# Seven products of halves for the first projection of both MLPs, with the weight sums made by accumulating DMAs

## The chip, the cores and the metric

The kernel runs on one core of a Trainium2 chip. The core has a matrix engine (TensorE, PE in the profile, with its weight loads as PEld), a vector engine (VectorE, DVE), an activation engine (ScalarE, ACT), GpSimd (POOL) and SyncE (SP). SP and POOL also issue DMAs, from queues of their own. The metric is the device time of one execution in microseconds (us); lower is better.

## The reference

A trunk of two residual layers over 512 tokens of width 1024, all float32. Each layer is a token mixer and an MLP, both behind an RMS norm. Only the MLP's computation is touched:

```python
def rmsnorm(x, g):
    xf = x.astype(jnp.float32)
    y = xf * lax.rsqrt(jnp.mean(xf * xf, axis=-1, keepdims=True) + EPS)
    return (y * g.astype(jnp.float32)).astype(x.dtype)

def mlp(h, w1, w2):            # w1: 1024 x 4096, w2: 4096 x 1024
    a = jax.nn.relu(h @ w1)
    return (a * a) @ w2

for i in range(DEPTH):         # DEPTH = 2: an even mixer, then an odd one
    ...
    h = rmsnorm(x, norm_mlp[i])
    x = x + mlp(h, w1[i], w2[i])
```

## The kernel before

All activations lie transposed, features on the 128 partitions and 512 tokens along the row. A float32 product is made of three matmuls in a rounded 32-bit format: each operand is split into a high part and the remainder, and `mm3` (L124) adds high by high, high by low and low by high.

Weights come as blocks of 128 x 1024, in the order in which they are used. `block_parts` (L101) loads block i from HBM by a DMA on SP's queue into `raw` (two buffers), ACT copies it into `whi` (L111) and DVE subtracts that from `raw` into `wlo` (L112); `whi` and `wlo` have four buffers each. This is called the split of a block below. `wblock` (L119) hands out the next block and has two more under way in the program text. Apart from the even mixer, where the order of TensorE is written by hand, the framework orders the instructions of each engine when it compiles, by the order of the text and by when its model expects their operands.

An MLP (`mlp`, L301) alternates between two kinds of unit, each of two weight blocks, 48 matmuls with 512 columns into a PSUM tile of two banks:

- `m1(g)` (L319), four units for 8 of the 32 feature tiles of the hidden layer. `Norm.step` (L294) has written the inputs, x times the norm's gain, split into A[0:8] and A[8:16]. The factor of the norm per token, `rs`, comes behind the product: DVE takes max(o, 0) * rs (L326), ACT squares it (L327) and makes the high part (L329), DVE the low part (L330).
- `m2(g)` (L345), four units that multiply those 8 hidden tiles with w2 and add to x (`x_add`, L287). In the last round (g = 3) each unit is followed by the steps of the next norm, or by the store to HBM. The very last unit (`last_unit`, L332) is cut finer, and its last half into two products of 256 columns.

The order is m1(0), m1(1), m2(0), m1(2), m2(1), m1(3), m2(2), m2(3). Before an MLP stands the last projection of the mixer (units `woa` in the even one, `wo1` in the odd one), after each unit of which two steps of the MLP's norm follow.

Of the kernel before, what the change touches and what calls it, by code (L numbers as in the profile page):

```python
# [7 lines left out]
F32 = mybir.dt.float32  # L8
F32R = mybir.dt.float32r
# [10 lines left out]
WARM = 17  # L20
LAT = (4.56, 2.32, 3.03, 2.9, 2.44)
GLAT = (0.88, 0.94, 1.37, 0.54, 2.0)

V_MIX = 0
V_MLP = 16
# [19 lines left out]
def kernel(  # L45
# [45 lines left out]
    def mm_tile(name):  # L91
        return ps.tile([P, 2, S], F32, tag="mm", name=name, bufs=2)
# [4 lines left out]
    wcount = [0]  # L97
    ready = []
    AHEAD = 2

    def block_parts(n):  # L101
        i = wcount[0]
# [12 lines left out]
    def emit_block():  # L115
        for _ in block_parts(1):
            pass

    def wblock():  # L119
        while len(ready) < AHEAD + 1 and wcount[0] < w.shape[0]:  # L120
            emit_block()
        return ready.pop(0)

    def mm3(o, w_hi, w_lo, a_hi, a_lo, start, stop, swap=False):  # L124
        if swap:
            w_hi, w_lo, a_hi, a_lo = a_hi, a_lo, w_hi, w_lo
        pe.matmul(o, w_hi, a_hi, start=start, stop=False)  # L127
        pe.matmul(o, w_hi, a_lo, start=False, stop=False)  # L128
        pe.matmul(o, w_lo, a_hi, start=False, stop=stop)  # L129

    def t_unit_g(name, acts):
        o = mm_tile(name)
        n = len(acts)
        for b in range(n // 4):
            hi, lo = wblock()
            hi = hi.rearrange("p (k n) -> p k n", k=4)
            lo = lo.rearrange("p (k n) -> p k n", k=4)
            for kk in range(4):
                k = b * 4 + kk
                for j in range(2):  # L140
                    c = slice(j * P, (j + 1) * P)
                    mm3(o[:, j, :], hi[:, kk, c], lo[:, kk, c], A[:, acts[k][0], :], A[:, acts[k][1], :],
                        k == 0, k == n - 1)
                if k < n - 1:
                    yield
        return o
# [8 lines left out]
    def t_unit(name, acts):  # L155
        return drain(t_unit_g(name, acts))
# [126 lines left out]
    def bc2(t):  # L283
        return t[:, None, :].to_broadcast([P, 2, S])

    def x_add(o, n):
        dve.tensor_add(x[:, 2 * n : 2 * n + 2, :], x[:, 2 * n : 2 * n + 2, :], o)  # L287

    class Norm:
# [8 lines left out]
        def rs(self):  # L298
            return norm_rs(self.ss, self.name)

    def mlp(l, nrm, nxt):  # L301
        with ExitStack() as c2:
            mp = c2.enter_context(tc.tile_pool(name=f"mp{l}", bufs=2, reuse_waits="tile"))
            E = mp.tile([P, 16, S], F32R, tag="E", name=f"E{l}", bufs=1)
            st = {}

            def aslot(f):
                i = f % 8
                if (f // 8) % 2 == 0:
                    return A[:, 16 + i, :], A[:, 24 + i, :]  # L310
                return E[:, i, :], E[:, 8 + i, :]

            def apair(f):
                i = f % 8
                if (f // 8) % 2 == 0:
                    return A[:, 16 + i : 18 + i, :], A[:, 24 + i : 26 + i, :]
                return E[:, i : i + 2, :], E[:, 8 + i : 10 + i, :]

            def m1(g):  # L319
                for q in range(4):  # L320
                    f = 8 * g + 2 * q
                    o = t_unit(f"m1_{l}_{f}", H)
                    if "rs" not in st:
                        st["rs"] = nrm.rs()
                    r = mp.tile([P, 2, S], F32, tag="r", name=f"r_{l}_{f}")
                    dve.scalar_tensor_tensor(r, o, 0.0, bc2(st["rs"]), op0=ALU.max, op1=ALU.mult)  # L326
                    act.activation(r, r, AF.Square)  # L327
                    hi, lo = apair(f)
                    act.copy(hi, r)  # L329
                    dve.tensor_sub(lo, r, hi.bitcast(F32))  # L330

            def last_unit(g, n):  # L332
                ws = [[t.rearrange("p (k n) -> p k n", k=4) for t in wblock()] for _ in range(2)]
                for j, c0, c1 in ((0, 0, S), (1, 0, S // 2), (1, S // 2, S)):
                    c = slice(j * P, (j + 1) * P)
                    row = 2 * n + j
                    o = m_tile(f"m2_{l}_{g}_{n}_{j}_{c0}", "tp" if c0 else "s")
                    for k in range(8):
                        hi, lo = ws[k // 4]
                        ah, al = aslot(8 * g + k)  # L340
                        mm3(o[:, c0:c1], hi[:, k % 4, c], lo[:, k % 4, c], ah[:, c0:c1], al[:, c0:c1], k == 0, k == 7)
                    dve.tensor_add(x[:, row, c0:c1], x[:, row, c0:c1], o[:, c0:c1])
                    nc.sync.dma_start(out[row * P : (row + 1) * P, c0:c1], x[:, row, c0:c1])

            def m2(g):  # L345
                for n in range(4):
# [3 lines left out]
                    o = mm_tile(f"m2_{l}_{g}_{n}")  # L350
                    for b in range(2):
                        hi, lo = wblock()
                        hi = hi.rearrange("p (k n) -> p k n", k=4)
                        lo = lo.rearrange("p (k n) -> p k n", k=4)
                        for kk in range(4):
                            k = 4 * b + kk
                            ah, al = aslot(8 * g + k)
                            for j in range(2):
                                c = slice(j * P, (j + 1) * P)
                                mm3(o[:, j, :], hi[:, kk, c], lo[:, kk, c], ah, al, k == 0, k == 7)  # L360
# [8 lines left out]
            m1(0)  # L369
            m1(1)  # L370
            m2(0)
            m1(2)
            m2(1)
            m1(3)
            m2(2)
            m2(3)

    def even_mixer(nrm, nxt):
        nonlocal x
# [461 lines left out]
        plan.run(gla, fg)  # L841
        for _ in fg:
            pass
        woa = [t_unit_g(f"woa{n}", O[0:4]) for n in range(4)]
        for n in (0, 0, 1, 1):
            next(woa[n])
        for n in range(4):
            x_add(drain(woa[n]), n)
            nxt.step(2 * n)
            nxt.step(2 * n + 1)  # L850
        order.close()
        ops.close()

    def odd_mixer(nrm, nxt):
        with ExitStack() as c2:
# [44 lines left out]
            for c in range(2):  # L900
# [22 lines left out]
            for n in range(4):  # L923
                x_add(t_unit(f"wo1_{n}", O[4:8] + O[0:4]), n)
                nxt.step(2 * n)
                nxt.step(2 * n + 1)

    n0 = Norm("n0", V_MIX)
    n1 = Norm("n1", V_MLP)
    even_mixer(n0, n1)  # L930
    n2 = Norm("n2", V_MIX + 8)
    mlp(0, n1, n2)
    n3 = Norm("n3", V_MLP + 8)
    odd_mixer(n2, n3)
    mlp(1, n3, None)


def _t_block(np, w, k0, n0, width):
    per = 1024 // width
    return w[k0 : k0 + per * P, n0 : n0 + width].reshape(per, P, width).transpose(1, 0, 2).reshape(P, 1024)  # L940


def _pair(np, blocks, w, ks, n0):
    for k0 in ks:
        blocks.append(_t_block(np, w, k0, n0, 256))


def _layout(np, i):
# [8 lines left out]
            blocks.append(_t_block(np, we, 256 * b, n0, 512))  # L957

    def mlp(l):
        def m1(g):  # L960
            for q in range(4):
                _pair(np, blocks, w1[l], (0, 512), (8 * g + 2 * q) * P)

        def m2(g):
            for n in range(4):
                _pair(np, blocks, w2[l], (1024 * g, 1024 * g + 512), 256 * n)

        m1(0), m1(1), m2(0), m1(2), m2(1), m1(3), m2(2), m2(3)

    tok(kb), tok(qb), tok(vb)  # L970
    _pair(np, blocks, we, (0, 512), qa)
# [88 lines left out]
```

## Time and profile before

| | |
|---|---|
| median of 3 runs | 1088.49 us (1087.35 to 1090.71) |
| the profiled execution | 1089.53 us, of which the span from its first to its last instruction is 1087.5 us |
| mean granted TensorE clock | 0.998 of full speed |
| busy share of the span: PE, PEld, DVE, ACT, POOL | 99%, 82%, 51%, 37%, 10% |
| read from HBM, written | 101.94 MB, 2.10 MB |

The span is what the trace covers; the 2 us beside it belong to the execution's time. Matmuls are pipelined, so their durations overlap, and the pace of TensorE is read from the distance between the starts of consecutive matmuls.

### The profile page before, as it was taken

What the parts mean: (1) busy time and instruction counts of PE and PEld (TensorE: products, weight loads), DVE (VectorE), ACT (ScalarE), POOL (GpSimd) and SP (SyncE); (2) the same over time, 40 slices, a digit from 0 to 9 for tenths busy, and PEclk for the clock granted to TensorE, in tenths of its full rate; (3) what the DMA queues carried; (4) which work ended last, traced back from release to release, by engine and by line L of the source; (5) the groups of instructions that cost most, each with busy time, mean ns of one, the idle gap of its engine ahead of it and who ended that gap; (6) DMA issues with size and microseconds to landing.
All of it is one profiled execution on the core that took longest, in us unless ns stands there. A gap on an engine that the chain in (4) does not pass through costs nothing.

```text
span 1087.5 us, 12594 instructions
## 1 busy us (share of the span) xinstructions
PE 1076.5 (99%) x5008; PEld 889.8 (82%) x5008; DVE 556.0 (51%) x774; ACT 404.7 (37%) x554; POOL 113.2 (10%) x126
## 2 busy tenths in 40 slices
PE   9999999999999999999999999999999999999998
PEld 7678888688888888888888888888888888888887
DVE  6788875867444334334335774545443334344331
ACT  5465565545333133123224432334342133133110
POOL 2244523213000000000002100121000000000000
PEclk9999999999999999999999999999999999999999
DMA  7223114122222222323232322232323322323231
GB/s 230 79 78 97 59 61 152 40 78 97 97 97 97 97 97 97 97 97 97 97 97 97 107 97 89 97 98 89 99 95 99 95 99 96 97 96 99 95 112 58
DMA packets 32044, 104.84 MB, mean 96 GB/s; under 512 B 3730, under 2 KB 6259, under 8 KB 31987
## 3 DMA queue, kind: packets, MB, share of 16 engines
q1 hardware_dynamic: 31202, 101.69, 28.5%
q0 software_dynamic: 640, 2.10, 0.6%
q8 instruction: 39, 0.64, 0.3%
q10 hardware_dynamic: 144, 0.26, 0.1%
q14 instruction: 19, 0.15, 0.0%
HBM read 101.94 MB, written 2.10 MB: 96 GB/s over the span
## 4 chain that ended last, share of the span: by engine, by line
PE 89%; DVE 5%; ACT 2%; POOL 1%; DMA 1%; issue 1%; SPq 0%; POOLq 0%; DVEq 0%; ACTq 0%
PE m L129 21%; PE m L128 21%; PE m L127 21%; PE wo L129 1%; PE wo L128 1%; PE wo L127 1%; DMA raw<-in_w_dram 1%; PE av L696 1%; PE ptp L677 1%; DVE wlo L112 1%; PE va L127 1%; PE va L129 1%; PE va L128 1%; PE xc L129 1%; PE xc L127 1%
## 5 line engine op out<-in xcount | busy, mean ns | idle before, releaser
L111 ACT CAST whi<-raw 128x1024 fp32r<-128x1024 f32 (+1 forms) x188 | 194.3, 1034 | 535.9 <-PE m L128 432.0
L112 DVE TENSOR_TENSOR wlo<-raw,whi 128x1024 fp32r<-128x1024 f32 (+1 forms) x188 | 228.0, 1213 | 198.4 <-ACT whi L111 198.2
L127 PE MATMUL m<-A,whi 128*128 128x512 f32 x768 | 299.0, 389 | 0.0
L129 PE MATMUL m<-A,wlo 128*128 128x512 f32 x768 | 299.0, 389 | 0.0
L128 PE MATMUL m<-A,whi 128*128 128x512 f32 x768 | 299.0, 389 | 0.0
L128 PEld LDWEIGHTS m<-A,whi 128*128 128x128 f32 x768 | 144.2, 188 | 30.0
L127 PEld LDWEIGHTS m<-A,whi 128*128 128x128 f32 x768 | 144.2, 188 | 29.9
L129 PEld LDWEIGHTS m<-A,wlo 128*128 128x128 f32 x768 | 144.2, 188 | 29.7
L128 PE MATMUL m<-E,whi 128*128 128x512 f32 (+1 forms) x264 | 101.1, 383 | 0.0
L129 PE MATMUL m<-E,wlo 128*128 128x512 f32 (+1 forms) x264 | 101.1, 383 | 0.0
L127 PE MATMUL m<-E,whi 128*128 128x512 f32 (+1 forms) x264 | 101.1, 383 | 0.0
L287 DVE TENSOR_TENSOR x<-x,m 128x1024 f32<-128x1024 f32 x31 | 37.9, 1221 | 109.1 <-PE m L129 109.1
L326 DVE SCALAR_TENSOR_TENSOR r<-m,rs_n 128x1024 f32<-128x1024 f32 x32 | 39.2, 1225 | 96.8 <-PE m L129 96.7
L268 POOL TENSOR_TENSOR ss_n<-ss_n,sq_n 128x512 f32<-128x512 f32 x21 | 32.8, 1561 | 391.7 <-ACT sq_n L266 391.0
L127 PEld LDWEIGHTS m<-E,whi 128*128 128x128 f32 x264 | 49.6, 188 | 9.8
L128 PEld LDWEIGHTS m<-E,whi 128*128 128x128 f32 x264 | 49.6, 188 | 9.7
L129 PEld LDWEIGHTS m<-E,wlo 128*128 128x128 f32 x264 | 49.6, 188 | 9.6
L327 ACT ACTIVATE r<-r 128x1024 f32<-128x1024 f32 x32 | 34.0, 1061 | 19.9 <-DVE r L326 19.9
L330 DVE TENSOR_TENSOR E<-r,E 128x1024 fp32r<-128x1024 f32 x16 | 19.6, 1226 | 17.2 <-ACT E L329 17.2
L257 DVE SCALAR_TENSOR_TENSOR A<-x,vc,A 128x512 fp32r<-128x512 f32 x24 | 27.3, 1139 | 1.3
L330 DVE TENSOR_TENSOR A<-r,A 128x1024 fp32r<-128x1024 f32 x16 | 19.6, 1225 | 15.1 <-ACT A L329 15.1
L129 PE MATMUL wo<-A,wlo 128*128 128x512 f32 x64 | 24.9, 389 | 0.0
(299 smaller groups left out, 1422.7 us busy)
## 6 DMA issues: line engine op xcount, KB each, us to landing
raw<-in_w_dram SPq DMA_DIRECT2D x180, 512.0 KB, 3.3
xin<-in_xT_dram SPq DMA_DIRECT2D x16, 128.0 KB, 3.4
raw<-in_w_dram SPq DMA_DIRECT2D x8, 256.0 KB, 3.8
x<-in_xT_dram POOLq DMA_DIRECT2D x8, 256.0 KB, 6.2
out_dram<-x SPq DMA_DIRECT2D x7, 256.0 KB, 2.0
cn<-in_con_dram SPq DMA_DIRECT2D x1, 736.0 KB, 6.4
pw<-in_poolw_dram ACTq DMA_DIRECT2D x1, 256.0 KB, 2.7
out_dram<-x SPq DMA_DIRECT2D x2, 128.0 KB, 1.7
```

Source lines behind the costliest of these rows:

```text
L111: act.copy(hi[:, c], raw[:, c])
L112: dve.tensor_sub(lo[:, c], raw[:, c], hi[:, c].bitcast(F32))
L127: pe.matmul(o, w_hi, a_hi, start=start, stop=False)
L128: pe.matmul(o, w_hi, a_lo, start=False, stop=False)
L129: pe.matmul(o, w_lo, a_hi, start=False, stop=stop)
L257: dve.scalar_tensor_tensor(A[:, 8 + k, c], src[:, k, c], col(gcol + k), A[:, k, c].bitcast(F32), op0=ALU.mult, op1=ALU.subtract)
L268: (dve if first else pool).tensor_add(ss, ss, sq)
L287: dve.tensor_add(x[:, 2 * n : 2 * n + 2, :], x[:, 2 * n : 2 * n + 2, :], o)
L326: dve.scalar_tensor_tensor(r, o, 0.0, bc2(st["rs"]), op0=ALU.max, op1=ALU.mult)
L327: act.activation(r, r, AF.Square)
L330: dve.tensor_sub(lo, r, hi.bitcast(F32))
L677: pe.transpose(tp[:, c : c + P], hs[h, i][:, j * P : (j + 1) * P], ident)
```

## The change

The first projection of both MLPs is computed in groups of four hidden tiles (512 features). Its inner dimension (even and odd tiles of x), its features (two pairs of tiles) and its tokens (two halves of 256) are each cut in two, and the 2 x 2 by 2 x 2 block product is made from seven products in place of eight (the Strassen-Winograd scheme).

- Sums on the side of x: `Mlp.step` replaces `Norm.step` before an MLP. For two tiles of x, ACT makes the four halves times the gain, DVE four sums and differences of 256 columns; the seven operands of 256 columns are split by one ACT copy and one DVE subtraction over 1792 columns.
- Sums on the side of w1: `sum_block` replaces `block_parts` for these blocks. Seven weight operands are made of four blocks per group. Three start as plain loads on SP's queue (x, y and z in `SUMS`), the other four are made by a DMA on POOL's queue that adds a block of HBM to the tile in SBUF (`accum_op`), after the previous sum in that tile has been split. Each of the seven is split as before.
- Products: `group` runs seven products of 24 matmuls with 256 columns. ACT copies two of the results out of PSUM, DVE makes seven sums of 128 x 512, and `finish` applies Relu and the square (two ACT passes), the high part (ACT) and the low part (DVE), twice per group with 128 x 1024. In the first group, `early` interleaves the first four products.
- The norm's factor: since relu(rs h)^2 = rs^2 relu(h)^2, the factor is squared once and applied behind the second projection: `down` is a DVE product and a DVE sum in place of `x_add`.
- Order: groups 0, 1, 2, m2(0), 3, 4, m2(1), 5, 6, m2(2), 7, m2(3). In m2(3) the first halves of units 0 and 1 come first.

```diff
+    SUMS = (("x", 3, True), ("y", 0, True), ("x", 2, False), ("y", 2, False), ("x", 0, False), ("z", 1, True),
+            ("x", 1, False))
+    def split_w(raw, i):
+        hi = wp.tile([P, 1024], F32R, tag="whi", name=f"whi{i}")
+        lo = wp.tile([P, 1024], F32R, tag="wlo", name=f"wlo{i}")
+        ready.append((hi, lo))
+        act.copy(hi, raw)
+        dve.tensor_sub(lo, raw, hi.bitcast(F32))
+
+    def sum_block(n):
+        i = wcount[0]
+        which, q, fresh = SUMS[n]
+        if not fresh:
+            nc.gpsimd.dma_start(chain[which], w[i + q], accum_op=ALU.add)
+        else:
...
+            nc.sync.dma_start(chain[which], w[i + q])
+        split_w(chain[which], f"{i}_{n}")
...
+    class Mlp:
...
+        def step(self, n):
+            e = self.T[:, n % 2 * 2048 : (n % 2 + 1) * 2048]
...
+            for j, i in ((0, 6), (1, 0)):
+                k = 2 * n + j
+                act.activation(half(i, 2), x[:, k, :], AF.Copy, scale=col(self.gcol + k))
+            dve.tensor_sub(half(3), half(7), half(1))
+            dve.tensor_sub(half(2), half(6), half(7))
+            dve.tensor_sub(half(4), half(3), half(6))
+            dve.tensor_add(half(5), half(4), half(0))
+            hi, lo = (t[:, n, :] for t in self.B)
+            act.copy(hi, e[:, 0:NB])
+            dve.tensor_sub(lo, e[:, 0:NB], hi.bitcast(F32))
+            for k in (2 * n, 2 * n + 1):
+                sumsq(self.ss, k, self.name, x)
...
+            def pieces(o, hi, lo, slot, us=(0, 1), ks=(0, 1, 2, 3)):
+                for u in us:
+                    for k in ks:
+                        c = slice((4 * u + k) * P, (4 * u + k + 1) * P)
+                        ah, al = (t[:, k, slot * HALF : (slot + 1) * HALF] for t in nrm.B)
+                        mm3(o[:, u * HALF : (u + 1) * HALF], hi[:, c], lo[:, c], ah, al, k == 0, k == 3)
+
+            def group(f0):
...
+                def finish(j):
+                    t = r[:, j::2, :]
+                    act.activation(t, t, AF.Relu)
+                    act.activation(t, t, AF.Square)
+                    hi, lo = (v[:, j::2, :] for v in agroup(f0))
+                    act.copy(hi, t)
+                    dve.tensor_sub(lo, t, hi.bitcast(F32))
...
+                if f0 == 0:
+                    early = [(o, *wblock(), slot) for o, slot in ((m4, 5), (m1, 6), (m5, 2), (m7, 3))]
+                    for us, ks in (((0,), (0, 1, 2)), ((0,), (3,)), ((1,), (0, 1, 2, 3))):
+                        for args in early:
+                            pieces(*args, us, ks)
+                    act.copy(c11, wide(m1))
+                    act.copy(es, wide(m5))
+                else:
+                    product(m4, 5)
+                    product(m1, 6)
+                    act.copy(c11, wide(m1))
+                    product(m5, 2)
+                    act.copy(es, wide(m5))
+                    product(m7, 3)
+                m6 = m_tile(f"m6_{nm}", "s")
+                product(m6, 4)
+                dve.tensor_add(c21, wide(m6), c11)
+                dve.tensor_sub(c22, wide(m7), c21)
+                dve.tensor_add(c12, c21, es)
+                dve.tensor_add(c21, wide(m4), c22)
+                dve.tensor_sub(c22, c22, es)
+                finish(1)
+                m2_ = m_tile(f"m2_{nm}", "tp")
+                product(m2_, 0)
+                dve.tensor_add(c11, wide(m2_), c11)
+                m3 = m_tile(f"m3_{nm}", "av")
+                product(m3, 1)
+                dve.tensor_add(c12, wide(m3), c12)
+                finish(0)
+                if "rs" not in st:
+                    st["rs"] = rs = nrm.rs()
+                    dve.tensor_mul(rs, rs, rs)
+
+            def down(n, o, c=slice(0, S), j=slice(0, 2)):
...
+                dve.tensor_mul(t, o, st["rs"][:, None, c].to_broadcast([P, m, c.stop - c.start]))
+                dve.tensor_add(xs, xs, t)
...
-                    x_add(o, n)
...
+                    m2_part(o, g, 1)
+                    down(n, o)
...
+            for g, hs_ in enumerate(((0, 1, 2), (3, 4), (5, 6), (7,))):
+                for h in hs_:
+                    group(4 * h)
+                m2(g)
```

## Rows read from the trace of the kernel before

**Rows 1.** The page's busy time, share of the span and instructions of each engine.

```profile
PE 1076.5 (99%) x5008; PEld 889.8 (82%) x5008; DVE 556.0 (51%) x774; ACT 404.7 (37%) x554; POOL 113.2 (10%) x126
```

**Rows 2.** Windows inside each MLP: busy us (instructions), clock, DMA share, GB/s.

```profile
300.00:400.00 100.00, 100.00 (x443) 82.85 (x442) 39.60 (x33) 29.80 (x30) 0.00 (x0) 1.00 0.30 100
800.00:900.00 100.00, 100.00 (x442) 82.81 (x442) 39.52 (x34) 30.59 (x29) 0.00 (x0) 1.00 0.30 97
```

**Rows 3.** The chain that ended last, shares of the span by engine.

```profile
PE 89%; DVE 5%; ACT 2%; POOL 1%; DMA 1%; issue 1%; SPq 0%; POOLq 0%; DVEq 0%; ACTq 0%
```

**Rows 4.** Timeline, PE and PEld, last m2 units: start us, us, instruction.

```profile
1054.82 0.39 PE L129 MATMUL m<-E,wlo 128*128 128x512 f32 x1
...
1077.94 0.39 PE L129 MATMUL m<-E,wlo 128*128 128x512 f32 x1
1078.16 0.28 PE L127 MATMUL m<-E,whi 128*128 128x256 f32 x1
1078.17 0.19 PEld L128 LDWEIGHTS m<-E,whi 128*128 128x128 f32 x1
...
1078.28 0.19 PEld L129 LDWEIGHTS m<-E,wlo 128*128 128x128 f32 x1
...
1083.80 0.28 PE L129 MATMUL m<-E,wlo 128*128 128x256 f32 x1
```

**Rows 5.** Groups by line and form: busy us, mean ns; idle before, releaser.

```profile
L111 ACT CAST whi<-raw 128x1024 fp32r<-128x1024 f32 x180 | 189.4, 1053 | 532.0 <-PE m L128 432.0 <-PE wo L128 20.4 <-PE xc L128 13.3
L327 ACT ACTIVATE r<-r 128x1024 f32<-128x1024 f32 x32 | 34.0, 1061 | 19.9 <-DVE r L326 19.9
L702 ACT COPY lo<-av 64x512 f32<-64x512 f32 x8 | 4.7, 584 | 4.0 <-PE av L696 3.9
...
L112 DVE TENSOR_TENSOR wlo<-raw,whi 128x1024 fp32r<-128x1024 f32 x180 | 221.7, 1232 | 194.5 <-ACT whi L111 194.4
L326 DVE SCALAR_TENSOR_TENSOR r<-m,rs_n 128x1024 f32<-128x1024 f32 x32 | 39.2, 1225 | 96.8 <-PE m L129 96.7
L287 DVE TENSOR_TENSOR x<-x,m 128x1024 f32<-128x1024 f32 x31 | 37.9, 1221 | 109.1 <-PE m L129 109.1
L274 DVE TENSOR_TENSOR ss_n<-ss_n,ss_n 128x512 fp32r<-128x512 f32 x4 | 2.8, 691 | 3.8 <-ACT ss_n L273 3.7
```

**Rows 6.** DMA queues and issues, and the source line of POOL's DMAs.

```profile
q1 hardware_dynamic: 31202, 101.69, 28.5%
...
raw<-in_w_dram SPq DMA_DIRECT2D x180, 512.0 KB, 3.3
...
x<-in_xT_dram POOLq DMA_DIRECT2D x8, 256.0 KB, 6.2
...
L747 POOL DMA_DIRECT2D x<-in_xT_dram x8: 536/536/748, 162.8 to 166.7; - x8
...
DMA to landing us min/median/max: 4.3/6.2/7.8
```

**Rows 7.** Timeline of ACT and DVE at the end of an m1 unit.

```profile
307.31 1.05 ACT L111 CAST whi<-raw 128x1024 fp32r<-128x1024 f32 x1 [4.38 <-PE m L128]
308.80 1.06 ACT L327 ACTIVATE r<-r 128x1024 f32<-128x1024 f32 x1 [0.43 <-DVE r L326]
...
307.54 1.23 DVE L326 SCALAR_TENSOR_TENSOR r<-m,rs_n 128x1024 f32<-128x1024 f32 x1 [3.36 <-PE m L129]
```

**Rows 8.** Timeline around the ends of the mixers, and at the end of the kernel.

```profile
239.09 1.22 DVE L287 TENSOR_TENSOR x<-x,woa 128x1024 f32<-128x1024 f32 x1 [5.33 <-PE woa L129]
...
253.75 1.21 DVE L287 TENSOR_TENSOR x<-x,woa 128x1024 f32<-128x1024 f32 x1
...
735.19 1.22 DVE L287 TENSOR_TENSOR x<-x,wo 128x1024 f32<-128x1024 f32 x1 [3.35 <-PE wo L129]
...
736.45 0.72 ACT L256 ACTIVATE A<-x,vc 128x512 fp32r<-128x512 f32 x1 [0.43 <-DVE x L287]
...
1084.11 0.42 DVE L342 TENSOR_TENSOR x<-x,m 128x256 f32<-128x256 f32 x1 [2.45 <-PE m L129]
```

More of the change, by code (lines that the diff above doesn't have):

```diff
@@ L99 @@
     AHEAD = 2
+    HALF = S // 2
+    NB = 7 * HALF
+    SUMS = (("x", 3, True), ("y", 0, True), ("x", 2, False), ("y", 2, False), ("x", 0, False), ("z", 1, True),
+            ("x", 1, False))
+    todo = list(_order())
+    chain = {}
+    def split_w(raw, i):
[10 more added lines that the diff above has]
+        else:
+            if which == "z":
+                chain[which] = wp.tile([P, 1024], F32, tag="raw", name=f"raw{i + q}", bufs=2)
+            else:
+                chain[which] = chain["pool"].tile([P, 1024], F32, tag=f"sum{which}", name=f"sum{which}{i}", bufs=2)
+            nc.sync.dma_start(chain[which], w[i + q])
+        split_w(chain[which], f"{i}_{n}")
+        if n == 6:
+            wcount[0] += 4
     def block_parts(n):
+        assert todo.pop(0) is None
         i = wcount[0]
@@ L115, in emit_block @@
     def emit_block():
-        for _ in block_parts(1):
-            pass
+        if todo[0] is None:
+            for _ in block_parts(1):
+                pass
+        else:
+            sum_block(todo.pop(0))
     def wblock():
-        while len(ready) < AHEAD + 1 and wcount[0] < w.shape[0]:
+        while len(ready) < AHEAD + 1 and todo:
             emit_block()
@@ L299, in rs, with __init__, half @@
             return norm_rs(self.ss, self.name)
+    class Mlp:
+        def __init__(self, l, gcol):
+            self.l, self.gcol, self.name = l, gcol, f"m{l}"
+            self.stack = ExitStack()
+            self.mp = mp = self.stack.enter_context(tc.tile_pool(name=f"mp{l}", bufs=1, reuse_waits="tile"))
+            chain["pool"] = mp
+            ext = mp.tile([P, 4 * NB + 64], F32R, name=f"ext{l}")
+            self.T = mp.tile([P, 8 * S], F32, tag="E", name=f"T{l}")
+            flat = A.rearrange("p a s -> p (a s)")
+            off = (flat[:, LEAN : LEAN + 4 * NB], ext[:, LEAN : LEAN + 4 * NB])
+            self.B = [t.rearrange("p (k n) -> p k n", k=4) for t in off]
+            self.ss = np_.tile([P, S], F32, tag="ss", name=f"ss_{self.name}", bufs=1)
+            self.got = 0
+        def step(self, n):
+            e = self.T[:, n % 2 * 2048 : (n % 2 + 1) * 2048]
+            def half(i, m=1):
+                return e[:, i * HALF : (i + m) * HALF]
+            for j, i in ((0, 6), (1, 0)):
[10 more added lines that the diff above has]
+                sumsq(self.ss, k, self.name, x)
+        def rs(self):
+            return norm_rs(self.ss, self.name)
@@ L301, in mlp, with agroup @@
     def mlp(l, nrm, nxt):
-        with ExitStack() as c2:
-            mp = c2.enter_context(tc.tile_pool(name=f"mp{l}", bufs=2, reuse_waits="tile"))
-            E = mp.tile([P, 16, S], F32R, tag="E", name=f"E{l}", bufs=1)
+        with nrm.stack:
+            mp = nrm.mp
+            E = mp.tile([P, 8, S], F32R, tag="E", name=f"E{l}")
             st = {}
+            def agroup(f0):
+                t, i = ((A, 16), (A, 24), (E, 0))[f0 // 4 % 3]
+                return t[:, i : i + 4, :], t[:, i + 4 : i + 8, :]
@@ L307, in aslot @@
             def aslot(f):
[L308 to L330, printed above, removed]
+                return [t[:, f % 4, :] for t in agroup(f)]
@@ L349, in m2 @@
                         return
[L350 to L360, printed above, removed]
-                    x_add(o, n)
+                    if g < 3 or n > 1:
+                        o = mm_tile(f"m2_{l}_{g}_{n}")
+                        m2_part(o, g, 0)
+                    elif n == 0:
+                        for i in range(2):
+                            o = mm_tile(f"m2_{l}_{g}_{i}")
+                            m2_part(o, g, 0)
+                            held.append(o)
+                    if held:
+                        o = held.pop(0)
+                    m2_part(o, g, 1)
+                    down(n, o)
                     if g == 3:
@@ L843, in even_mixer @@
             pass
+        ops.close()
+        nxt = Mlp(*nxt)
         woa = [t_unit_g(f"woa{n}", O[0:4]) for n in range(4)]
@@ L922, in odd_mixer, with _order @@
                 dve.tensor_sub(A[:, 24 + 2 * c : 26 + 2 * c, :], y, A[:, 16 + 2 * c : 18 + 2 * c, :].bitcast(F32))
[L923 to L926, printed above, removed]
+        nxt = Mlp(*nxt)
+        for n in range(4):
+            x_add(t_unit(f"wo1_{n}", O[4:8] + O[0:4]), n)
+            nxt.step(n)
+        return nxt
     n0 = Norm("n0", V_MIX)
-    n1 = Norm("n1", V_MLP)
-    even_mixer(n0, n1)
+    n1 = even_mixer(n0, (0, V_MLP))
     n2 = Norm("n2", V_MIX + 8)
     mlp(0, n1, n2)
-    n3 = Norm("n3", V_MLP + 8)
-    odd_mixer(n2, n3)
+    n3 = odd_mixer(n2, (1, V_MLP + 8))
     mlp(1, n3, None)
+def _order():
+    m1, m2 = tuple(range(7)), 8 * (None,)
+    mlp = 3 * m1 + m2 + 2 * m1 + m2 + 2 * m1 + m2 + m1 + m2
+    return 32 * (None,) + mlp + 24 * (None,) + mlp
 def _t_block(np, w, k0, n0, width):
@@ L945, in _pair, with _group @@
         blocks.append(_t_block(np, w, k0, n0, 256))
+def _group(np, blocks, w, f0):
+    v = w.reshape(4, 2, P, w.shape[1])
+    for j in range(2):
+        for h in range(2):
+            c = [v[:, h, :, (f0 + 2 * u + j) * P : (f0 + 2 * u + j + 1) * P] for u in range(2)]
+            blocks.append(np.stack(c).transpose(2, 0, 1, 3).reshape(P, 1024))
 def _layout(np, i):
@@ L959, in mlp @@
     def mlp(l):
[L960 to L968, printed above, removed]
+        for g, hs in enumerate(((0, 1, 2), (3, 4), (5, 6), (7,))):
+            for h in hs:
+                _group(np, blocks, w1[l], 4 * h)
+            parts = [(n, b) for n in range(4) for b in range(2)]
+            if g == 3:
+                parts[1:3] = parts[2:0:-1]
+            for n, b in parts:
+                _pair(np, blocks, w2[l], (1024 * g + 512 * b,), 256 * n)
     tok(kb), tok(qb), tok(vb)
```

44 lines of the change are left out of this document (32 added, 12 removed).

## The prediction

> **What bounds the kernel now.** I read the busy line first: PE is busy 99% of the span, DVE half, ACT a third [rows 1]. That is a share of modelled durations, so I look at the chain that ended last (PE 89% of it [rows 3]) and at windows inside each MLP (PE without a gap, DVE 40%, ACT 30%, DMA engines 30% [rows 2]). Then the pace, from the starts of matmuls in the timeline [rows 4]. From 1054.82 to 1077.94 lie 102 steps of 512 columns: 23.12/102 = 0.2267 us each. So the MLPs are bound by the number of matmuls times their pace; everything else is covered. DVE and ACT wait for PE: the high part of a weight block sits idle 532 us before its 180 instructions, 432 us of it until a PE matmul frees the buffer [rows 5].
>
> The order on ACT matters later. At 307.31 a split starts, the moment PE has done with a block, and the square of the unit that ended with it comes at 308.80 [rows 7]. In the program text that split stands after the square. So the compiler has reordered, and a split runs as soon as the buffer four blocks back is free: weights have a lead of three blocks.
>
> **The change, part by part.**
>
> *Matmuls.* Before, four hidden tiles take 96 matmuls of 512 columns: 96 x 0.2267 = 21.76 us. After, seven products of 24 with 256 columns. The last half unit shows these: 47 steps from 1078.16 to 1083.80, 0.1200 us each, while a weight load of 0.19 us starts every 0.12 us, so loads overlap and don't set the pace [rows 4]. 168 x 0.12 = 20.16 us, 1.60 less. Break-even is 0.1295 per matmul. Two MLPs of eight groups: 16 x 1.60 = 25.6 us. One product now lasts 2.88 us, a weight block before lasted 5.44. The lead of three blocks shrinks from 16.3 to 8.64 us.
>
> *ACT and DVE in a group of 20.16 us.* By [rows 5]: ACT seven high parts at 1.05, two copies out of PSUM at 0.58, two finishes of Relu, square and copy (1.06 + 1.06 + 1.05): 7.4 + 1.2 + 6.3 = 14.9 us (74%; before 8.4 of 21.8). DVE seven low parts at 1.23, seven sums of 512 at 0.69, two low parts of the hidden tiles at 1.23: 8.6 + 4.8 + 2.5 = 15.9 us (79%). Both fit, but no longer with ease: the five sums behind the fifth product (3.5 us) and both finishes on ACT (6.3 us) fall together at a group's end, and a split behind them has 8.64 - 2.4 = 6.2 us to spare (2.4 is its own 1.05 + 1.23 and handovers). If all of both finishes goes first, after waiting for the sums, it is late by up to about 3 us. Bounds nothing to 3 us per group; I take a quarter of a us, 4 us in all, because the compiler moves splits ahead [rows 7].
>
> *Weight sums.* A group loads 7 x 0.52 MB in place of four; 48 more blocks are 25 MB in all. The DMA engines took 28.5% of 1087.5 us for 101.69 MB [rows 6], so 1.6 us a block: 11.2 of 20.2 us in a group. No adding DMA is in the trace. Its time from issue to landing, L, is bounded below by SP's plain block, 3.3 us. POOL's 256 KB took at least 4.3, of which 0.54 is POOL's own, and half a block more is 0.8: 5.1. If the add has to read the tile as well, another 1.6: 6.7 [rows 6]. Nothing excludes either end; I take the middle, L = 5.0.
>
> What L may be follows from the chain x, four splits with three adds between, since an add waits for the split before it. A link is L + 2.4. The next group's first split comes 1.2 us behind the last, so a sustained group needs 3(L + 2.4) + 1.2, and falls behind PE's 20.16 by 3L - 11.8: 3.2 us at L = 5.0. The first group after an m2 stretch has slack. Its third split is done 3.0 us before the group starts (the buffer is freed 5.44 before), the seventh 2(L + 2.4) later, and it is needed at 6 x 2.88 = 17.3: slack 15.5 - 2L, 5.5 us at 5.0. Runs of groups are 3, 2, 2, 1. A second group loses 3.2 of 5.5, nothing shows; the third stalls PE by 0.9, twice in the kernel: 2 us. Queued behind a waiting add on POOL are only the next adds; the norm's sums run there only near the mixers.
>
> *Start of an MLP.* Before, steps of the norm were covered by 36 matmuls of 512, 8.2 us. Now the last step is longer: sum into x 1.22, two ACT copies 1.4, four DVE sums of 256 at 0.42, ACT copy of 1792 columns about 1.7, DVE subtraction about 2.0 (scaled from 512 and 1024 columns): 8 us after the mixer's last product, plus a weight split of 1.2 on DVE [rows 5, 8]. The first half-product covers 36 x 0.12 = 4.3 us, the second halves another 4.3 if the compiler pulls them forward. Odd mixer: 0 to 5, I take 2.5. Even mixer: its units last 5.44, but DVE needs 1.2 + 1.2 + 1.7 + 2.0 = 6.1 per step, four from 239.09 on, so about 263.5, where the products start at about 253 [rows 8]: 2 to 6.3, I take 4. Together 6.5.
>
> *The norm's factor.* A product of 1.22 per m2 unit on DVE, 32 times: covered, since a unit lasts 10.9 us and DVE then has 2 x 1.23 + 2.44 to do. If not covered it would stall only at an MLP's end. The kernel's last sum gets one product of 256 more: +0.4 [rows 8]. The wait of the first m1 evacuation for `rs` goes; PE did not stall there [rows 2], so it returns nothing.
>
> Sum: -25.6 + 4 + 2 + 6.5 + 0.4 = -12.7. Against the profiled execution, 1089.5 - 12.7 = 1076.8; the median lies 1.0 below that execution, so **1076 us**.
>
> **The rivals.**
>
> *The adds arrive too late.* An add that reads the tile too moves 2 x 1.6 us through the engines; L = 6.1 or more, and the engines fill to 3 x 1.6 + 4 x 3.2 = 17.6 of 20.2 us, so that loads queue. Then a following group loses 6.5 with a slack of 3.3: 3.2 in each of two runs, 9.7 in the run of three, 16.1 an MLP, 32 in all where the sum has 2. Time 1106; at L = 7 (9.2 lost, slack 1.5) 32 an MLP, 1138. From L = 5.6 on (7 an MLP) the kernel is slower than before. For it: both operands must be read somewhere; against it: the second read is of SBUF, and the engines are 30% busy now [rows 2].
> The Trainium skill states such a rule (Collectives: The Full Stack, "The bandwidth ceiling: the fold count and why AG ≠ RS ≠ AR"): a reduce runs at half the rate of a copy, because it reads two sources through one ring. By that rule L is at the upper end here; no run before shows an adding DMA.
>
> *ACT and DVE set the pace.* If the order fixed at compile time puts the finishes ahead of splits, 1.5 us more per group costs 24: 1100. For it 74% and 79% busy; against it [rows 7].
>
> *No gain per product.* If 256-column matmuls run at 0.13 between changing banks and buffers, 16 x 168 x 0.01 = 27 us are lost: 1103. Against it 47 steps without one slow [rows 4].
>
> **How the numbers follow.** Forecast 0.52, adds too late 0.30, ACT and DVE 0.13, no gain 0.05. The forecast's own range is 1063 (nothing but 25.6 gained, 0.4 lost) to 1084. Of the rivals' 0.48 I leave the upper part of the first out, 0.14, and 0.04 below: 1064 to 1116. About 0.3% (3 us) is what a measurement can tell from no change. Faster: the forecast and 0.05 of the rivals, 0.57; same 0.09 (an L near 5.5, or one us more a group); slower 0.34.
>
> **What would show it.** Matmuls at 0.12 in all groups, 6160 of them; PE gaps only at the start of an MLP and in third groups; ACT near 74%, DVE near 79% in group windows; 127 MB read. The adds' time to landing decides: under 5.5 right, above 6 wrong, and the gaps then stand before the products of x in second and third groups, released by an ACT split that waited for a DMA. Gaps behind ACT with the DMA long landed would mean the second rival.

## The result, and the profile after

The changed kernel is slower: 1130.26 us median of 4 runs (1128.22 to 1131.36) against 1088.82 for the kernel before beside it, a ratio of 1.0377 (95% interval 1.0355 to 1.04). The forecast was 1076 us in a range of 1064 to 1116, and faster.

The page after, against [rows 1] and [rows 3]: the busy line, and the chain that ended last.

```profile
PE 1072.5 (95%) x6160; PEld 933.9 (83%) x6160; DVE 698.7 (62%) x962; ACT 502.6 (44%) x674; POOL 168.6 (15%) x190
```

```profile
PE 58%; DMA 14%; issue 11%; DVE 8%; ACT 6%; POOL 2%; SPq 0%; POOLq 0%; ACTq 0%; DVEq 0%
```

PE's busy share fell by only 4 points, but PE's share of the chain fell from 89% to 58%, and DMA has 14% of it in place of 1%. Windows say where. The four below are the first group of the first MLP, the two groups behind it, a later run of two, and the group that stands alone between two stretches of m2. The columns are those of [rows 2].

```profile
252.70:289.20 36.50, 26.28 (x171) 24.24 (x170) 24.47 (x26) 16.19 (x19) 9.96 (x7) 0.77 0.33 74
289.20:346.30 57.10, 48.00 (x340) 45.84 (x339) 34.07 (x39) 30.62 (x34) 6.12 (x7) 0.88 0.62 133
389.30:434.10 44.80, 41.98 (x337) 41.13 (x336) 26.36 (x29) 20.88 (x23) 4.37 (x5) 0.96 0.62 142
564.20:584.00 19.80, 19.80 (x169) 19.76 (x169) 11.83 (x12) 7.06 (x8) 0.88 (x1) 1.00 0.42 99
```

The lone group shows what the change can do: no gap, a clock of 1.00 and 19.80 us, 1.96 less than the four hidden tiles took before. Timeline of PE, its first and its last matmul:

```profile
564.26 0.28 PE L160 MATMUL dc<-A,whi 128*128 128x256 f32 x1
...
583.93 0.28 PE L162 MATMUL m<-A,wlo 128*128 128x256 f32 x1
```

167 steps in 19.67 us are 0.1178 us a matmul. From the first matmul to that of the next group or of the next m2, the groups take, in the first MLP, 36.5, 57.25, 44.87, 42.96 and 19.8 us (runs of 1, 2, 2, 2 and 1), in the second 28.3, 54.3, 42.7, 45.0 and 19.8: 391.5 us in all. At 19.8 a group it would be 316.8. So 31 us are gained and 75 lost again: 25 in the two first groups, 32 in the two groups behind them, 17 in the four later runs of two. The net, 44, is near the measured 41.

The DMA queues (packets, MB, share) and the sums' row in the list of issues, against [rows 6]:

```profile
q1 hardware_dynamic: 28898, 93.30, 25.4%
q0 software_dynamic: 9856, 35.66, 18.4%
...
sumx<-in_w_dram POOLq DMA_DIRECT2D x48, 512.0 KB, 5.5
```

The adding DMAs by their source line (POOL's time in ns min/median/max, first and last start; then the landing):

```profile
L119 POOL DMA_DIRECT2D sumx<-in_w_dram x48: 864/873/930, 242.0 to 1067.2; - x48
...
DMA to landing us min/median/max: 5.2/5.5/6.9
```

A plain block (0.524 MB) on q1 takes 25.4% x 1129.4 / 93.30 x 0.524 = 1.61 us of all engines, as before. On q0 are 64 adds and eight loads of x (some 6 us): (207.8 - 6.4)/64 = 3.15 us an add, twice a plain block. The waits that answer to it (us in total, times, longest):

```profile
DVE wlo L113 <- ACT whi L112: 151.8, 61, 6.2
ACT whi L112 <- DMA sumx<-in_w_dram: 122.4, 27, 7.1
PE m L160 <- ACT whi L112: 12.2, 12, 1.9
```

ACT waits 122 us for sums, 27 times, and up to 7.1 us at once; PE waits behind it for high parts. A link of the chain x is the way from the start of one add to the start of the next. Two links in the second group behind the first, in the timelines of POOL, ACT and DVE:

```profile
315.16 0.88 POOL L119 DMA_DIRECT2D sumx<-in_w_dram  x1 [9.24 <-DVE wlo L113]
324.19 0.88 POOL L119 DMA_DIRECT2D sumx<-in_w_dram  x1 [5.22 <-DVE wlo L113]
333.53 0.87 POOL L119 DMA_DIRECT2D sumx<-in_w_dram  x1 [8.47 <-DVE wlo L113]
...
320.64 1.06 ACT L409 ACTIVATE r<-r 128x1024 f32<-128x1024 f32 x1
321.60 1.03 ACT L112 CAST whi<-sumx 128x1024 fp32r<-128x1024 f32 x1
...
330.93 1.04 ACT L112 CAST whi<-sumx 128x1024 fp32r<-128x1024 f32 x1 [2.19 <-DMA sumx<-in_w_dram]
...
322.67 1.23 DVE L113 TENSOR_TENSOR wlo<-sumx,whi 128x1024 fp32r<-128x1024 f32 x1 [0.67 <-ACT whi L112]
```

The adds start 9.03 and 9.34 us apart. With 5.5 to landing the first was there at about 320.7; ACT was in a finish pass and came to the high part at 321.60, DVE to the low part at 322.67, and POOL to the next add at 324.19, when that was done. The second link had no queue: ACT stood waiting, and its sum came only at 330.9, 6.7 us after the add's start. In a later run of two most links are like this one:

```profile
394.84 0.87 POOL L119 DMA_DIRECT2D sumx<-in_w_dram  x1 [7.50 <-DVE wlo L113]
404.39 0.87 POOL L119 DMA_DIRECT2D sumx<-in_w_dram  x1 [8.67 <-DVE wlo L113]
412.63 0.87 POOL L119 DMA_DIRECT2D sumx<-in_w_dram  x1 [4.30 <-DVE wlo L113]
421.94 0.87 POOL L119 DMA_DIRECT2D sumx<-in_w_dram  x1 [8.45 <-DVE wlo L113]
...
410.02 1.05 ACT L112 CAST whi<-sumx 128x1024 fp32r<-128x1024 f32 x1 [5.43 <-DMA sumx<-in_w_dram]
...
411.11 1.23 DVE L113 TENSOR_TENSOR wlo<-sumx,whi 128x1024 fp32r<-128x1024 f32 x1 [2.15 <-ACT whi L112]
```

From 404.39 to 412.63 are 8.24 us: 5.6 until ACT starts, the two passes, and 0.3 to the next add. Inside groups that follow another the links take 8.1 to 9.7 us. From the third add of a group (394.84) to that of the next (421.94) are 27.1 us; over the eight such pairs it is 26.2 to 28.5.

The start of the first MLP, in timelines of DVE, POOL and PE, where [rows 8] stood:

```profile
250.27 1.21 DVE L320 TENSOR_TENSOR x<-x,woa 128x1024 f32<-128x1024 f32 x1
253.54 0.42 DVE L360 TENSOR_TENSOR T<-T 128x256 f32<-128x256 f32 x1
253.88 1.84 DVE L361 TENSOR_TENSOR T<-T 128x256 f32<-128x256 f32 x1
255.75 1.38 DVE L362 TENSOR_TENSOR T<-T 128x256 f32<-128x256 f32 x1
258.19 5.04 DVE L365 TENSOR_TENSOR ext<-T,A 128x1792 fp32r<-128x1792 f32 x2
268.59 2.03 DVE L365 TENSOR_TENSOR ext<-T,A 128x1792 fp32r<-128x1792 f32 x1 [1.21 <-ACT A L364]
...
248.15 3.35 POOL L301 TENSOR_TENSOR ss_m<-ss_m,sq_m 128x512 f32<-128x512 f32 x2 [0.50 <-ACT sq_m L299]
253.86 2.99 POOL L301 TENSOR_TENSOR ss_m<-ss_m,sq_m 128x512 f32<-128x512 f32 x2
...
260.25 0.58 PE L161 MATMUL dc<-ext,whi 128*128 128x256 f32 x1 [3.94 <-DVE ext L365]
260.63 0.41 PE L162 MATMUL dc<-A,wlo 128*128 128x256 f32 x1
...
261.91 0.41 PE L162 MATMUL m<-A,wlo 128*128 128x256 f32 x1
```

A DVE sum of 256 columns takes 0.42 us, but 1.84 and 1.38 beside POOL's sums of squares from 253.86 on; L320, with one operand in PSUM, keeps its 1.21 beside POOL's sums from 248.15 on. The last of the four splits ends at 270.6. PE waits 3.94 us for the low part of an operand, and then steps at (261.91 - 260.63)/6 = 0.213 us: the granted clock, 0.77 over the first group, is here at the lower of its two levels (1.2 and 2.4 GHz).

The trace of the kernel before had already shown this, on L257, whose inputs lie in SBUF. The second of these two DVE rows lies beside a sum on POOL from 242.80 to 244.11, and takes twice as long:

```profile
241.36 0.75 DVE L257 SCALAR_TENSOR_TENSOR A<-x,vc,A 128x512 fp32r<-128x512 f32 x1
...
243.16 1.50 DVE L257 SCALAR_TENSOR_TENSOR A<-x,vc,A 128x512 fp32r<-128x512 f32 x1
```

### The profile page after: what moved, and what is told of

Read it like the earlier page. It is cut to its first block, busy times and chain, and to the rows that moved or that the text cites. A ratio compares the mean times of both kernels' runs of the same rounds, so it can differ in the third digit from the quotient of the medians.

```text
span 1129.4 us, 15386 instructions
## 1 busy us (share of the span) xinstructions
PE 1072.5 (95%) x6160; PEld 933.9 (83%) x6160; DVE 698.7 (62%) x962; ACT 502.6 (44%) x674; POOL 168.6 (15%) x190
## 3 DMA queue, kind: packets, MB, share of 16 engines
q1 hardware_dynamic: 28898, 93.30, 25.4%
## 4 chain that ended last, share of the span: by engine, by line
PE 58%; DMA 14%; issue 11%; DVE 8%; ACT 6%; POOL 2%; SPq 0%; POOLq 0%; ACTq 0%; DVEq 0%
PE m L162 11%; PE m L160 11%; PE m L161 11%; DMA sumx<-in_w_dram 11%; DVE wlo L113 3%; DMA raw<-in_w_dram 2%; ACT whi L112 2%; PE wo L161 1%; PE wo L160 1%; PE wo L162 1%; PE av L830 1%; PE ptp L811 1%; DVE wlo L142 1%; PE va L160 1%; PE va L162 1%
## 5 line engine op out<-in xcount | busy, mean ns | idle before, releaser
L160 PE MATMUL m<-A,whi 128*128 128x256 f32 (+1 forms) x1032 | 335.4, 325 | 14.0 <-ACT whi L112 12.2
L162 PE MATMUL m<-A,wlo 128*128 128x256 f32 (+1 forms) x1032 | 335.7, 326 | 6.3 <-DVE wlo L113 6.2
L142 DVE TENSOR_TENSOR wlo<-raw,whi 128x1024 fp32r<-128x1024 f32 (+1 forms) x124 | 151.3, 1223 | 55.8 <-ACT whi L141 54.9
L161 PE MATMUL m<-ext,whi 128*128 128x256 f32 x640 | 183.6, 287 | 0.0
L113 DVE TENSOR_TENSOR wlo<-sumx,whi 128x1024 fp32r<-128x1024 f32 x64 | 78.3, 1224 | 139.3 <-ACT whi L112 138.9
L161 PE MATMUL m<-A,whi 128*128 128x512 f32 (+1 forms) x392 | 150.9, 385 | 0.0
L161 PEld LDWEIGHTS m<-ext,whi 128*128 128x128 f32 x640 | 125.4, 196 | 0.0
L160 PE MATMUL dc<-A,whi 128*128 128x256 f32 x256 | 76.0, 297 | 11.1 <-ACT whi L112 6.5
L161 PEld LDWEIGHTS m<-A,whi 128*128 128x128 f32 x392 | 73.7, 188 | 14.5
L161 PE MATMUL dc<-ext,whi 128*128 128x256 f32 x256 | 76.1, 297 | 7.1 <-DVE ext L365 7.1
L162 PE MATMUL dc<-A,wlo 128*128 128x256 f32 x256 | 76.2, 298 | 4.5 <-DVE wlo L113 4.5
```

The lines of the kernel that those rows point to most:

```text
L113: dve.tensor_sub(lo, raw, hi.bitcast(F32))
```

## The experiments

Theory A: the sums arrive too late, since an add takes the engines twice as long and a link of the chain is longer than I took it. Theory B: ACT and DVE have too much to do in a group. Theory C: the start of an MLP costs more than 6.5 us, for DVE and POOL hold each other up. Experiments e1 to e9 ran once; the kernel before took 1090.56 us beside e1 to e4, 1089.65 beside e5 to e8, and 1089.56 (7 runs) beside e9 and the first of the timed ones.

**e1, plain loads in the chain's place.**

```diff
-            nc.gpsimd.dma_start(chain[which], w[i + q], accum_op=ALU.add)
+            nc.gpsimd.dma_start(chain[which], w[i + q])
```

> The four adding DMAs of a group load without adding: same queue, same waits, same order on every engine; the weight sums are left out of the computation. Theory A (the adds arrive too late, because an add takes the DMA engines twice as long): time to landing falls from 5.5 to about 4, a link of the chain from about 9 to 7.5 us, and of the 50 us lost in groups other than the first of each MLP some 25 come back: about 1105. Theory B (the load on ACT and DVE and its order at a group's end): 1130 as before. Theory C (the start of an MLP) concerns 25 us that stay in either case.

1093.67 us, 36.6 less, which is more than I expected, with every wait and every engine's order as before. Its list of issues:

```profile
sumx<-in_w_dram POOLq DMA_DIRECT2D x48, 512.0 KB, 3.8
```

Its window of the two groups behind the first:

```profile
287.10:334.60 47.50, 41.74 (x342) 39.94 (x341) 33.39 (x39) 29.40 (x33) 3.69 (x7) 1.00 0.46 154
```

With 3.8 us to landing in place of 5.5 the later runs of two take 39.57 us, nothing lost; only the run behind the first group still loses 8.

**e2, no chain.** All seven operands are plain loads on SP's queue, in four buffers of their own.

```diff
-        if not fresh:
-            nc.gpsimd.dma_start(chain[which], w[i + q], accum_op=ALU.add)
...
+        chain[which] = chain["pool"].tile([P, 1024], F32, tag="sumx", name=f"sum{i}_{n}", bufs=4)
+        nc.sync.dma_start(chain[which], w[i + q])
```

> All seven weight operands of a group are loaded plainly by SP, each into a buffer of its own (four buffers), with no wait on the split before; the weight sums are left out of the computation. ACT, DVE and PE do all that they did. Theory A: groups other than the first of each MLP run at 19.8 us, all 50 us come back: about 1080, with the 25 us of the two starts still lost. Theory B: most of the 50 us stay lost, over 1115.

1078.08 us, 52.2 less. The window of groups 1 and 2:

```profile
288.00:326.00 38.00, 38.00 (x336) 37.91 (x335) 31.59 (x36) 27.14 (x32) 0.00 (x0) 1.00 0.58 190
```

DVE is busy 31.59 of 38.00 us (83%), ACT 27.14 (71%), and PE has no gap. So B falls as a bound: with every pass of ACT and DVE in place, PE sets the pace. The first groups still take 35.6 and 26.5 us.

**e3, Relu and Square left out of `finish`** (both ACT passes).

```diff
-                    act.activation(t, t, AF.Relu)
-                    act.activation(t, t, AF.Square)
```

> The two ACT passes Relu and Square are left out of both finishes, 4.2 us of ACT per group, so the hidden layer is not activated; the adding DMAs stay. Theory A: a split behind a finish waits about 1 us less per link, up to 10 us in all: 1120 to 1128. Theory B: the bursts on ACT halve and most of the 50 us come back: under 1095.

1115.09 us, 15 less: more than A alone said, far less than B said. The passes stand on ACT beside high parts of sums, as at 320.64 above, and lengthen links: the two that ACT's queue held at 9.66 us (from 295.39) and 9.03 us (from 315.16) take 7.86 and 8.10 here. But the adds also landed a little sooner, in e3 and in e4 (5.3 us in place of 5.5), in the later runs too, which the edits don't explain; so not all of the 15 us is shown to be the passes'.

**e4, the squares later.** The token norm's squares and sums come behind the first group, the sums on DVE.

```diff
-            for k in (2 * n, 2 * n + 1):
-                sumsq(self.ss, k, self.name, x)
...
         def rs(self):
+            for k in range(KT):
+                sq = self.ss if k == 0 else np_.tile([P, S], F32, tag="nt", name=f"sq_{self.name}{k}")
+                act.activation(sq, x[:, k, :], AF.Square)
+                if k > 0:
+                    dve.tensor_add(self.ss, self.ss, sq)
```

> The sums of squares of the MLP's norm are made behind the first group instead of within the steps, and their adds run on DVE instead of POOL; the result is the reference's. Theory C (the steps before an MLP end too late, DVE being slowed beside POOL's adds): the first groups of 36.5 and 28.3 us shorten by 5 to 8 us each, more where TensorE no longer falls to half its clock: 1110 to 1120. If POOL and the squares don't matter at the start: 1130.

1115.75 us, 14.5 less. The first groups went from 36.5 and 28.3 us to 30.6 and about 27, some 7 of it. The rest came behind them, almost all in the later runs of two, which hold nothing of what was moved; there it goes with the sooner landing.

**e5 to e8, shorter chains on top of e4.** In e5 the seventh operand is one DVE sum of two tiles on chip, so that the chain x has two adds.

```diff
+        if n == 6:
+            dve.tensor_add(chain["z"], chain["z"], chain["x"])
+            which = "z"
```

In e6 the third operand also has a tile of its own, filled ahead of its turn; e7 is e6 with that sum on POOL; e8 is e6 with two of the seven operands of x split later.

> On top of e4_squares_later (1115.8): the seventh weight operand of a group is made by a DVE addition of two tiles in SBUF in place of an adding DMA, so that two links of about 9 us are left in the chain of x in place of three, and DVE has 1.2 us more per group (86% of 19.8 us). Theory A: a group's chain takes about 24 us in place of 28, runs of two groups fit their slack, the third group of a run still loses about 5: 1080 to 1088. Rival: DVE is now the bound and the gain is small: over 1100.

> As e5_last_sum_dve, and the third operand gets a tile of its own (one plain load more per group, the add waits for that load alone and not for a split): one link between splits is left. Theory A: all groups but the first of each MLP run at 19.8 us, as in e2_no_chain, and the starts as in e4_squares_later: 1064 to 1070. Rival (DVE at 86%, or the DMA engines at 15.8 of 19.8 us per group, take the place of the chain): no better than e5_last_sum_dve.

> As e6_one_link with the seventh operand's addition on POOL in place of DVE. If DVE has room, POOL's longer addition (about 3 us by its 1.56 us for 512 columns) changes little, within 3 us of e6_one_link. If DVE was the bound there: faster by more than 3. If DVE is held up while POOL reads SBUF, as in the steps before an MLP: slower by more than 3.

> As e6_one_link, and the steps before an MLP split only the five of the seven token operands that the first products need (1280 columns in place of 1792); the two others are split straight from x while the first group runs. Theory C (the steps end too late): the first groups shorten by 1 to 3 us each: 2 to 6 us faster than e6_one_link. If the starts don't depend on DVE's and ACT's work in the last steps: no change.

1095.01, 1093.75, 1098.33 and 1091.98 us: the first two missed what I expected, e7 is 4.6 us slower than e6 (POOL's sum takes 2.43 us), and the 1.8 us by which e8 is faster are less than two runs of one kernel can differ by. From e5 on, later runs of two take 39.57 us, so two adds fit in a group and three don't. But groups 1 and 2 of the first MLP take 52.4 in e5 and 49.6 in e6. The timelines of POOL, ACT and PE there, in e6, and its row of adds in the list of issues:

```profile
279.50 0.87 POOL L127 DMA_DIRECT2D sumx<-in_w_dram  x1 [22.82 <-DMA sumx<-in_w_dram]
280.95 0.88 POOL L131 DMA_DIRECT2D sumy<-in_w_dram  x1 [0.58 <-DVE wlo L113]
...
290.56 1.05 ACT L112 CAST whi<-sumy 128x1024 fp32r<-128x1024 f32 x1 [6.54 <-DMA sumy<-in_w_dram]
291.51 2.00 ACT L422 ACTIVATE r<-r 128x1024 f32<-128x1024 f32 x2
293.42 1.99 ACT L423 ACTIVATE r<-r 128x1024 f32<-128x1024 f32 x2
...
298.66 0.57 ACT L444 COPY es<-m 128x512 f32<-128x512 f32 x1
...
299.29 0.38 PE L172 MATMUL m<-A,whi 128*128 128x256 f32 x1 [3.51 <-ACT es L444]
...
sumx<-in_w_dram POOLq DMA_DIRECT2D x32, 512.0 KB, 7.2
```

ACT stands 6.54 us before the high part of a late sum; finish passes and the next group's copy out of PSUM (`es`) are queued behind it, and PE waits 3.51 us for that copy. That sum was issued 1.45 us behind another add and came about 9.6 us later. Over the whole of e6 an add of x takes 7.2 us to landing in place of 5.5. So the shorter chain brought the adds closer together, and each of them took longer. That speaks for one half of the rival that e6's expectation named, the DMA engines, which no run tests by itself; its other half, DVE as a bound, isn't seen in the later runs.

**e9, no chain and the squares later** (e2 and e4 together).

> No sum is made at all (all seven operands are plain loads, so the weights' sums are left out), and the token norm's squares come behind the first group with their additions on VectorE: the two edits that by themselves returned 52 us and 14.5 us. If the two losses, late sums and the crowded start of an MLP, are separate and are all of the loss, the sixteen groups keep most of their 31 us: 1060 to 1068 us, with groups 1 and 2 at 38 us and the first groups at 28 and 25 us or less. If they are one loss seen twice (VectorE and ScalarE simply have too much to do in the first 60 us of an MLP), the second edit returns little on top of the first: 1074 us or more.

1069.89 us, 60.4 less than the changed kernel, where the two by themselves sum to 66.7: mostly two losses, though 2 us above the range that I gave for that. Groups 1 and 2 take 38 us, the first groups 28.5 and 25.1. Those 14.0 us over 2 x 19.8 are what is left of the start.

**f1, the first group of each MLP plain**, with e5's sums and the squares behind it. The mixer's last steps write x times the gain, split, as in the kernel before; the sums of x for the later groups are made under that group's 96 matmuls of 512 columns. To make room for it some tiles lie elsewhere; the operands of x begin at their tile's first column, in place of column 48 (`LEAN`).

```diff
-    mlp = 3 * m1 + m2 + 2 * m1 + m2 + 2 * m1 + m2 + m1 + m2
+    mlp = 4 * (None,) + 2 * m1 + m2 + 2 * m1 + m2 + 2 * m1 + m2 + m1 + m2
...
+            def plain(f0):
...
+                for j in range(2):
...
+                    for n in (2 * j, 2 * j + 1):
+                        nrm.sums(n)
```

> The first group of each MLP goes back to eight products (512-column matmuls on the plain halves, which is all that the mixer's last steps then have to write), the sums of x for the other seven groups are made beneath it, the squares come behind it, and the seventh operand is the VectorE addition of two that are on chip. By the theory (late sums, and a start that asks ScalarE, VectorE and GpSimd for more than they do in the time) nothing of the loss is left: the start as in the kernel before, 14 groups at 1.96 us less each, so 27 us less than before, 1060 to 1068 us. By the rival (two groups in a row behind the first are the trouble, by the sums' DMAs, whatever the start is) those runs still lose some 10 us an MLP: 1078 to 1086 us.

1075.69 us median of 4 runs, 0.9876 of the kernel before (0.9856 to 0.9896): faster than both. Windows of the plain group, of groups 1 and 2, and of a later run of two:

```profile
251.50:273.20 21.70, 21.70 (x98) 17.97 (x97) 15.07 (x21) 13.12 (x16) 1.82 (x2) 1.00 0.38 79
273.20:318.70 45.50, 43.11 (x340) 42.27 (x339) 37.01 (x44) 29.33 (x36) 3.42 (x4) 0.96 0.52 128
362.20:402.60 40.40, 40.40 (x338) 40.36 (x337) 29.28 (x31) 21.03 (x23) 2.58 (x3) 1.00 0.60 139
```

Nothing is lost at the start. Its matmuls of 256 columns step at 0.1200 us, so a group takes 20.16: 14 x (21.76 - 20.16) = 22.4 gained, 5.1 and 4.6 lost in the two groups behind the first of each MLP, 12.7 net; measured 13.9. The time lies between the two ranges of the expectation, and each of its theories was half right: the start is cured, and the run behind it still loses.

**f2 and f3, the squares and the factor later still**: at the first place that needs the factor (f2), inside the third group (f3).

```diff
-                if "rs" not in st:
-                    st["rs"] = rs = nrm.rs()
-                    dve.tensor_mul(rs, rs, rs)
...
             def down(n, o, c=slice(0, S), j=slice(0, 2)):
+                if "rs" not in st:
+                    st["rs"] = rs = nrm.rs()
+                    dve.tensor_mul(rs, rs, rs)
```

> As the kernel with the first group plain, and the squares, their sum and the norm's factor are now emitted behind the two groups that follow it, at the first place that needs them. In that kernel the two groups took 45.3 and 44.8 us where later runs of two take 40.2; the stop was behind a cast of a late sum with finish passes, squares and the factor's products queued behind it. By that reading the two runs go to 40 to 42 us and the kernel to 1066 to 1071 us. By the rival, that the sums' own lateness in these two groups is enough, the runs stay at 44 us or more and the kernel at 1074 to 1077 us; a wait of the third projection's first results for the factor, which is a new wait, would show behind the run, at 1074 us or more too.

> As the two kernels before it, with the squares, their sum and the factor emitted inside the third group, behind the finish of its first half: later than where they held the two groups up by 5 us, earlier than where the third projection then waited 4 us for the factor. If the two waits are separate and there is room between them, both shrink: 1070 to 1074 us, with the runs of two at 42 us and no wait behind them. If ScalarE and VectorE have no room for them at all in these 40 us, one wait or the other stays, as a trade: 1075 to 1079 us.

1078.55 us (0.99 of before, 0.9881 to 0.9918) and 1078.43 (0.9901, 0.9881 to 0.9922). In f2 groups 1 and 2 do go from 45.4 and 44.9 (the two MLPs) to 41.6 and 41.1 us, and the wait that the third case named takes it back. PE, in the m2 unit behind them:

```profile
326.37 0.39 PE L165 MATMUL m<-A,wlo 128*128 128x512 f32 x1
330.19 0.50 PE L311 MATMUL nps_m<-ss_m,ones_r 128*128 128x512 f32 x1 [3.44 <-ACT ss_m L309]
```

In f3, in the same place:

```profile
323.60 0.39 PE L165 MATMUL m<-A,wlo 128*128 128x512 f32 x1
326.32 0.74 PE L311 MATMUL nps_m<-ss_m,ones_r 128*128 128x512 f32 x1 [2.34 <-ACT ss_m L309]
```

So it is a trade, at the three places that were tried: the squares delay the two groups or the factor that follows them.

## Why the prediction was wrong

*Matmuls:* right, a little small. 0.1178 us a matmul where I took 0.12, 1.96 a group for 1.60: 31 us gained for 25.6.

*Weight sums:* this is the step that failed, 2 us taken and 49 measured (32 and 17). The term that was mis-sized is the link, L + 2.4 = 7.4 us. Inside groups it took 8.1 to 9.7. L came out at 5.5 in the median (5.2 to 6.9); the median lies inside the bounds of 3.3 to 6.7, 0.5 above what I took, and by my formula 5.5 alone would have lost about 11 us. What stands beside L was 2.7 where ACT was free when the sum landed, and 3.4 (315.16) to 4.4 where it had other passes to do first, a queue that I had not given it.

The formula itself holds for the later runs, and it is steep: one us on the link adds 3 to a sustained group and takes 2 from the slack, so 5 for a run of two, 8 for a run of three, 36 in all. From third add to third add it gives 23.4 us with my link, and 26.2 to 28.5 passed. With the later runs' own links, about 8.3, and 26.5 between their third adds, a second group falls 26.5 - 19.8 = 6.7 behind, against a slack of 20.3 - 2 x 8.3 = 3.7 (the prediction's 15.5 - 2L, written for the link), and loses 3.0; the measured losses are 3.4 and 3.1 in two runs of two, and 5.3 and 5.4 in the two in which PE was also granted the lower clock for 3.4 us. The larger part, the 32 us of the two groups behind the first, has the longest links, ACT's queue and more of the lower clock together; no run takes these apart. Break-even was a link of 8.0, and I had it 0.6 below that.

The rival "the adds arrive too late" was what happened: two of its signs are in the rows, an add that takes twice a plain block's engine time and PE waiting for high parts whose ACT split had waited for a sum; e1 and e2 show the cause, 36.6 and 52.2 us back. I priced it by L alone, from L = 6.1, and the sign that I named (under 5.5 right, above 6 wrong) could not tell, at 5.5. The rule of the Trainium skill that I set beside it (Collectives: The Full Stack, "The bandwidth ceiling: the fold count and why AG ≠ RS ≠ AR"), a reduce at half the rate of a copy, stands there for collectives in a ring. The engine time of this local add agrees, 3.15 us against 1.61; what I concluded from it for L, the upper end, does not: 5.5.

*Start of an MLP:* 6.5 taken, 25 measured, the second term that failed. I summed DVE's durations as if POOL stood still: before the first MLP the steps were to end at about 263.5 and ended at 270.6. What part is POOL's is not separated. e4 returns some 7 us at the starts by moving the squares off POOL and out of the way, and e9 still loses 14.0 there. f1, with the short steps and the plain first group of the kernel before, loses none, which points to the longer steps; but e8, whose steps split five operands in place of seven, shortens one first group by 2.3 us (26.8 to 24.5) and the other not at all (28.9 to 29.2).

*ACT and DVE in a group:* as a bound, rightly kept small: e2 and e9 run at 83% and 71% busy without a gap. But "a split runs as soon as the buffer is free" was read from a kernel whose weights were never late. In an order fixed at compile time the high part of a late sum holds what stands behind it, as at 290.56 in e6.

*The norm's factor:* right. The m2 stretches take 43.5 us as before (192 x 0.2267), so its products are covered.

*What I left out:* behind some of its waits PE works at the lower clock; behind others it doesn't (in e1 it was idle for 5.8 of 47.5 us in groups 1 and 2 at a granted clock of 1.00). In the changed kernel it was granted 0.77 over 36.5 us and 0.88 over 57.1: 0.23 x 2 x 36.5 + 0.12 x 2 x 57.1 = 30 us at half clock in that MLP's first run, a cost of 15 us at most, contained in the losses above. No run separates it from the waits.

## What to carry to other kernels

A chain of accumulate, split, accumulate must be priced by its whole link, with the queue on every engine that it passes, against the time that the consumer gives it; here a link 0.7 to 2.3 us longer than I took it was enough, since by the formula each us of it costs 36. Fewer links (one of three adds replaced by a sum on chip), squares behind the start, and one group of the old form, under which the new operands are made, turned 3.8% slower into 1.2% faster. Work moved out of one full stretch needs an emptier one to go to, or the wait moves with it.

## What the runs showed of the hardware

An adding DMA from HBM into SBUF took 5.5 us to landing for 512 KB where a plain one on the same queue took 3.8, 3.15 us of all engines for 1.61, and 0.87 us of POOL's own time for 0.53. Where two adds were issued close together, as in e6, their time to landing rose to 7.2 us.

DVE operations with both inputs in SBUF took up to four times as long beside POOL's sums (0.42 to 1.84 us), one with an input in PSUM did not (1.21 us). The Trainium skill has it so (SBUF — State Buffer, "Who interferes with whom"): a VectorE instruction with two SBUF inputs contends with a GpSimd instruction that reads SBUF, one with at most one such input does not, outside the modes in which VectorE reads one input through both its ports. The rows agree.

The pace of 256-column matmuls at full clock was 0.1178 us in most runs, 0.1134 in groups 1 and 2 of e2 and e9, and 0.1200 in f1 to f3 and in the kernel before. Why is open; 0.1200 goes with operands that begin at the first column of their tile, the other two with column 48, which no run changes by itself.
